# Sharing the transfers' semaphores, and moving the last store's wait behind the section's exit

## The chip, the cores and the metric

The kernel runs on one core of one Trainium2 chip. The metric is the device time of one execution in microseconds (us). A run would be called slow if it were over 1.5% above the fastest of its kernel. The span in a profile is the time from the first to the last instruction of the kernel.

## The reference

```python
def setup_inputs():
    batch, m, k, n = 16, 512, 1024, 768
    return {"x": randn(batch, m, k), "weight": randn(k, n), "sub_value": randn(batch, m, n)}   # float32

def reference(x, weight, sub_value):
    return (np.matmul(x, weight) - sub_value).astype(np.float32)
```

The 8192 rows of `x` make 64 row tiles of 128. Each tile is cast to half precision, transposed (on TensorE, for some tiles on VectorE), multiplied with the weights, and VectorE subtracts `sub_value` from the product in place.

## The kernel before

Everything stands in one hand-synchronized section. Each engine has a list of instructions with waits and increments. SyncE issues all 39 transfers, and each takes a semaphore of its own:

```python
    ctx.enter_context(tc.tile_critical(no_gpsimd_drain=True))
    ...
    for name in ("ident", "idle", "w", "cast", "evac", "pair", "turn", "mul", "finish"):
        counter[name] = tc.alloc_semaphore(name)
    ...
    def issue():
        while todo:
            kind, at, n = todo[0]
            ...
            sem = tc.alloc_semaphore(f"{kind}{at}")
            ...
            if kind == "s":                              # sub_value over rows that were stored
                for t in need:
                    waits.append((landed["o", t], 16))
            ...
            for t in span:
                landed[kind, t] = sem
            sp.add(lambda ...: nc.sync.dma_start(out=here, in_=there), waits, (sem, 16))
```

The last transfers of the list store the output in smaller and smaller pieces, 4, 2, 1 and 1 tiles. At the end SyncE waits for every store, then the section ends:

```python
    for q in (sp, act, dve, pool):
        q.emit(q.ops)
    for t in range(n_mt):
        if t == 0 or landed["o", t] is not landed["o", t - 1]:
            nc.sync.wait_ge(landed["o", t], 16)
```

What follows is made by the framework. At the section's exit SyncE raises a signal, each engine drains and answers, and SyncE waits for the answers. Then comes a barrier of all engines, which GpSimd gathers and releases; GpSimd clears the range of all semaphores that the kernel took; a second barrier ends the program.

## Time and profile before

| | before |
|---|---|
| device time, first runs | 211.04, 211.59, 211.55 us |
| span of the profile | 209.4 us |
| TensorE busy | 198.4 us, 95% |
| share of the main DMA queue | 97.8% |
| last store: issued, landed | 205.43, 207.74 us |
| landing to end of span | 1.62 us |

The page gives the span, each engine's busy time, the busy tenths of 40 slices and the DMA queues. The rows to read for this change are the ones at the very end, by source line: L448 is the final waits, L129 the section's entry and exit, L482 the framework's barriers and the clear. A row by source gives engine, operation and count, then minimum, median and maximum of the duration in ns, then the first and last start in us. A `q` behind an engine's name means its sequencer. These views round starts to 0.1 us. Where this document gives three decimals, they are read from the single records of the same trace.

### The profile page before, as it was taken

The numbers are of one execution on the slowest core, as the hardware profiler recorded it, in microseconds if no ns is written. First come the engines' busy times: TensorE is split into PE (matmuls) and PEld (weight loads), VectorE is DVE, ScalarE is ACT, GpSimd is POOL, SyncE is SP. The second block draws the span as 40 slices with busy tenths as digits, with TensorE's granted clock in tenths as the row PEclk, the third lists the DMA queues.
The fourth block names the chain that finished last, engine by engine and source line by source line (L and its number), as shares of the span: only waits on it lengthen the run. The fifth ranks groups of instructions, "written<-read, shape, count | busy, mean of one in ns | idle before, by whom it ended". The sixth has DMA issues, their size and how long they took to land.

```text
span 209.4 us, 2456 instructions
## 1 busy us (share of the span) xinstructions
PE 198.4 (95%) x1250; PEld 80.4 (38%) x738; DVE 114.0 (54%) x186; ACT 112.9 (54%) x115; POOL 0.7 (0%) x6
## 2 busy tenths in 40 slices
PE   7998799999979999999999999999999999999990
PEld 2432244444333344344344334434434433444430
DVE  0242235106149849929956965992994795332231
ACT  2555665676396274655727629455572750765410
POOL 1000000000000000000000000000000000000000
PEclk9999999999999999999999999999999999999998
DMA  6999999999999999999999999999999999999994
GB/s 200 417 427 425 427 432 434 441 438 423 401 448 417 452 412 429 452 432 424 421 427 452 415 437 448 407 424 446 423 435 441 426 423 426 427 434 432 427 383 171
DMA packets 5626, 87.17 MB, mean 416 GB/s; under 512 B 624, under 2 KB 624, under 8 KB 2032
## 3 DMA queue, kind: packets, MB, share of 16 engines
q1 hardware_dynamic: 5616, 87.03, 97.8%
q8 instruction: 7, 0.11, 0.2%
q14 instruction: 3, 0.02, 0.0%
HBM read 61.87 MB, written 25.17 MB: 416 GB/s over the span
## 4 chain that ended last, share of the span: by engine, by line
PE 80%; DMA 6%; DVE 5%; ACT 4%; SPq 2%; issue 1%; ACTq 0%
PE po_b L175 71%; PE pt_b L289 10%; DMA x_ring<-in_x_dram 6%; DVE xtp_b L316 3%; ACT x_b L271 2%; ACT xt_b L296 1%; DVE so_ring L360 1%; SPq L223 1%; SPq L252 1%; ACT x16p_b L271 0%; SPq L482 0%; ACTq L56 0%; SPq L129 0%
## 5 line engine op out<-in xcount | busy, mean ns | idle before, releaser
L175 PE MATMUL po_b<-w_sb,xt_b 128*128 128x384 f16 x800 | 145.7, 326 | 1.5 <-ACT xt_b L296 1.5
L360 DVE TENSOR_TENSOR so_ring<-po_b,so_ring 128x768 f32<-128x768 f32 x64 | 60.7, 956 | 60.5 <-PE po_b L175 40.2
L296 ACT COPY xt_b<-pt_b 128x1024 f16<-128x1024 f16 x50 | 50.6, 1012 | 73.8 <-PE pt_b L289 73.1
L340 PEld LDWEIGHTS <-xt_b 128*128 128x128 f16 x400 | 39.2, 98 | 58.4 <-issue 52.9
L316 DVE STREAM_TRANSPOSE xtp_b<-x16p_b 32x256 f32<-32x256 f32 x112 | 48.8, 436 | 19.3 <-ACT x16p_b L271 17.4
L289 PE MATMUL pt_b<-ident,x_b 128*128 128x128 f32 x200 | 52.3, 274 | 2.7 <-ACT x_b L271 2.4
L271 ACT CAST x_b<-x_ring 128x1024 f16<-128x1024 f32 x50 | 51.6, 1048 | 5.9 <-DMA x_ring<-in_x_dram 5.9
L289 PEld LDWEIGHTS pt_b<-ident,x_b 128*128 128x128 f32 x200 | 27.6, 141 | 46.3 <-issue 40.4
L175 PE MATMUL po_b<-w_sb,xtp_b 128*128 128x384 f16 x224 | 42.9, 326 | 0.3 <-DVE xtp_b L316 0.3
L271 ACT CAST x16p_b<-x_ring 128x1024 f16<-128x1024 f32 x14 | 14.6, 1046 | 6.8 <-DMA x_ring<-in_x_dram 6.8
L340 PEld LDWEIGHTS <-xtp_b 128*128 128x128 f16 x112 | 11.0, 98 | 13.2 <-issue 11.2
L377 PE MATMUL po_b<-idle_x,idle_w 128*128 128x512 f16 x25 | 8.5, 496 | 1.5 <-DVE idle_x L371 1.5
L226 DVE CAST w_sb<-so_ring 128x768 f16<-128x768 f32 x8 | 4.1, 556 | 10.6 <-DMA so_ring<-in_weight_dram 10.6
L377 PEld LDWEIGHTS po_b<-idle_x,idle_w 128*128 128x128 f16 x25 | 3.0, 122 | 5.2 <-issue 3.0
L271 ACT ACT_TABLE_LOAD x1 | 1.3, 1283 | 0.9 <-SPq L129 0.9
L370 DVE MEMSET idle_w<- 128x64 uint32 x1 | 0.1, 112 | 1.0 <-SPq L129 1.0
L390 PE MATMUL po_b<-idle_x,idle_w 128*128 128x512 f16 x1 | 0.4, 379 | 0.0
L164 POOL TENSOR_SCALAR_AFFINE_SELECT ident<-ident 128x128 f32<-128x128 f32 x1 | 0.3, 292 | 0.1
L371 DVE MEMSET idle_x<- 128x256 uint32 x1 | 0.3, 272 | 0.0
L163 POOL MEMSET ident<- 128x128 f32 x1 | 0.2, 206 | 0.5 <-SPq L129 0.5
L390 PEld LDWEIGHTS po_b<-idle_x,idle_w 128*128 128x128 f16 x1 | 0.1, 98 | 0.2 <-issue 0.2
L471 POOL MEMSET const-bfloat16-1.0<- 128x1 bf16 x1 | 0.1, 102 | 0.0
(3 smaller groups left out, 0.3 us busy)
## 6 DMA issues: line engine op xcount, KB each, us to landing
so_ring<-in_sub_value_dram SPq DMA_DIRECT2D x7, 3072.0 KB, 24.3
out_dram<-so_ring SPq DMA_DIRECT2D x7, 3072.0 KB, 31.2
x_ring<-in_x_dram SPq DMA_DIRECT2D x5, 4096.0 KB, 22.7
x_ring<-in_x_dram SPq DMA_DIRECT2D x2, 2560.0 KB, 26.2
x_ring<-in_x_dram SPq DMA_DIRECT2D x3, 1536.0 KB, 22.4
so_ring<-in_weight_dram SPq DMA_DIRECT2D x4, 768.0 KB, 8.7
x_ring<-in_x_dram SPq DMA_DIRECT2D x3, 512.0 KB, 6.3
so_ring<-in_sub_value_dram SPq DMA_DIRECT2D x1, 1536.0 KB, 26.3
```

Source lines behind the costliest of these rows:

```text
L175: return nc.tensor.add_instruction(mybir.InstMatmult(name=nc.get_next_instruction_name(), engine=full.engine, ins=list(full.ins), outs=lis ...
L223: sp.add(lambda st=st, at=at: nc.sync.dma_start(out=st, in_=w_c[at]), then=(sem, 16))
L226: lambda at=at, r=r, st=st: nc.vector.tensor_copy(out=w_sb[:, at, r], in_=st[:, r]),
L252: sp.add(lambda here=here, there=there: nc.sync.dma_start(out=here, in_=there), waits, (sem, 16))
L271: act.add(lambda: nc.scalar.copy(out=to, in_=x_in), waits, count("cast"))
L289: pe.add(lambda: nc.tensor.transpose(words, from_, ident), waits, count("turn") if last else None)
L296: act.add(lambda: nc.scalar.copy(out=xt_b[:, d], in_=pt_b[:, b]), waits, count("evac"))
L316: dve.add(lambda: nc.vector.transpose(xt[b * Q : (b + 1) * Q, :, a * Q : (a + 1) * Q], x16[a * Q : (a + 1) * Q, :, b * Q : (b + 1) * Q],), ...
L340: pe.add(lambda weights=weights: nc.tensor.ldweights(weights, tile_position=(0, 0)), [w for w in waits if w[0] in ready])
L360: dve.add(lambda: nc.vector.tensor_tensor(out=o, in0=po[:, :, :NS], in1=o, op=mybir.AluOpType.subtract), [(landed["s", mi], 16), (counter[ ...
L377: lambda: nc.tensor.matmul(po_b[:, NPO - 1, 0], idle_w, idle_x, start=True, stop=True),
L390: pe.add(lambda: nc.tensor.matmul(po_b[:, NPO - 1, 0], idle_w, idle_x, start=True, stop=True), [(counter["ident"], 2)])
```

## The change

The intent: use fewer semaphores, so that less has to be cleared at the end, and let the exit's handshake between the engines run while the last store is still under way.

```diff
-    ctx.enter_context(tc.tile_critical(no_gpsimd_drain=True))
+    section = ctx.enter_context(ExitStack())
+    section.enter_context(tc.tile_critical(no_gpsimd_drain=True))
...
+    def lane(tag):
+        for one in lanes:
+            if one["tags"] <= known:
+                break
+        else:
+            one = {"sem": tc.alloc_semaphore(f"lane{len(lanes)}"), "value": 0, "tags": set()}
+            lanes.append(one)
+        one["value"] += 16
+        one["tags"].add(tag)
+        return one["sem"], one["value"]
...
-            sem = tc.alloc_semaphore(f"{kind}{at}")
...
+            sem, value = lane((kind, at))
             for t in span:
-                landed[kind, t] = sem
+                landed[kind, t] = (sem, value)
...
-    for t in range(n_mt):
-        if t == 0 or landed["o", t] is not landed["o", t - 1]:
-            nc.sync.wait_ge(landed["o", t], 16)
...
+    left = [one for one in lanes if not one["tags"] <= known]
+    last = next(one for one in left if of_o[n_mt - 1] in one["tags"])
+    for one in left:
+        if one is not last:
+            nc.sync.wait_ge(one["sem"], one["value"])
+    section.close()
+    with tc.tile_critical(sync_engine=mybir.EngineType.SP, no_gpsimd_drain=True):
+        nc.sync.wait_ge(last["sem"], last["value"])
```

A lane is a semaphore with a running count, and it is taken again only when all its transfers are known to be over; a wait names the count that was reached. The lines that keep `known` (a load is over when its tile was cast, a store when SyncE waited for it, and so on) are left out here. In the program as built, 39 transfer semaphores become 15 lanes, and the range that is cleared shrinks from 54 to 30 semaphores.

More of the change, by code (lines that the diff above doesn't have):

```diff
@@ L201 @@
     staged = {}
+    lanes = []
+    of_x, of_s, of_o = {}, {}, {}
+    known = set()
+    def lane(tag):
[8 more added lines that the diff above has]
+        return one["sem"], one["value"]
     def issue():
+        nonlocal known
         while todo:
@@ L226, in issue @@
                         lambda at=at, r=r, st=st: nc.vector.tensor_copy(out=w_sb[:, at, r], in_=st[:, r]),
-                        waits=[(sem, 16)], then=count("w"),
+                        waits=[(sem, value)], then=count("w"),
                     )
@@ L239, in issue @@
                 waits.append((counter["cast"], max(cast_at[t] for t in need)))
+                last = max(need, key=lambda t: cast_at[t])
+                known |= {tag for t, tag in of_x.items() if t in cast_at and cast_at[t] <= cast_at[last]}
             if kind == "s":
                 for t in need:
-                    waits.append((landed["o", t], 16))
+                    waits.append(landed["o", t])
+                    known.add(of_o[t])
                 for t in span:
@@ L245, in issue @@
                         waits.append((counter["w"], staged.pop(t % NSO)))
+                        known |= {("w", c) for c in w_at if w_at[c] <= waits[-1][1]}
             if kind == "o":
                 waits.append((counter["finish"], max(finish_at[t] for t in need)))
+                known |= {of_s[t] for t in finish_at if finish_at[t] <= max(finish_at[u] for u in need)}
+            sem, value = lane((kind, at))
             for t in span:
-                landed[kind, t] = sem
+                landed[kind, t] = (sem, value)
+                {"x": of_x, "s": of_s, "o": of_o}[kind][t] = (kind, at)
             if kind == "o":
@@ L258, in cast @@
         first = mi - mi % 2
-        waits = [(landed["x", mi], 16)]
+        waits = [landed["x", mi]]
         if first in ON_DVE:
@@ L361, in finish @@
             out=o, in0=po[:, :, :NS], in1=o, op=mybir.AluOpType.subtract
-        ), [(landed["s", mi], 16), (counter["mul"], mul_at[mi])], count("finish"))
+        ), [landed["s", mi], (counter["mul"], mul_at[mi])], count("finish"))
         finish_at[mi] = so_far["finish"]
```

## The prediction

> **What bounds the kernel now.** I read the page first: span, busy shares, the DMA row of the 40 slices, the chain that ended last.
>
> ```profile
> span 209.4 us, 2456 instructions
> ...
> PE 198.4 (95%) x1250; PEld 80.4 (38%) x738; DVE 114.0 (54%) x186; ACT 112.9 (54%) x115; POOL 0.7 (0%) x6
> ...
> DMA  6999999999999999999999999999999999999994
> ...
> q1 hardware_dynamic: 5616, 87.03, 97.8%
> ...
> PE 80%; DMA 6%; DVE 5%; ACT 4%; SPq 2%; issue 1%; ACTq 0%
> ```
>
> The reader is to see two resources full from the second slice to the last but one: TensorE 95% busy, and the DMA engines with packets during 97.8% of the span. The change adds, removes and resizes no transfer and no matmul, so it cannot shorten that body. What it can touch is the last slice, where the DMA row falls to 4.
>
> Next, the waits of the DMA queue in the last 3.5 us and the stores of the last 11 us.
>
> ```profile
> SPq L252 <- DVE so_ring L360: 2.2, 1, 2.2
> SPq L448 <- DMA out_dram<-so_ring: 1.7, 2, 0.9
> ```
> ```profile
> L252 SPq DMA_DIRECT2D out_dram<-so_ring x3: 332/333/333, 200.1 to 205.4; - x3
> ...
> DMA to landing us min/median/max: 2.3/4.0/5.7
> ```
>
> The last store is issued at 205.4 and lands 2.3 us later, at 207.7. SyncE meanwhile waits twice for landings, about 0.9 us each: until the store before the last is there, then until the last is. The last one's own 0.9 us is transfer time: it moves 384 KB, and 393,216 bytes at the page's mean 416 GB/s are 0.95 us.
>
> Then what stands between that landing and the end, by source line from 205.5 us on.
>
> ```profile
> L448 SPq EVENT_SEMAPHORE  x5: 28/28/28, 205.8 to 207.8; - x5
> ```
> ```profile
> L129 SPq EVENT_SEMAPHORE  x3: 17/28/28, 208.0 to 208.2; - x3
> L129 SPq COMPARE_BRANCH  x1: 32/32/32, 207.8 to 207.8; - x1
> ...
> L129 SPq DRAIN  x1: 7/7/7, 208.1 to 208.1; - x1
> L129 SPq NOP  x1: 13/13/13, 208.3 to 208.3; - x1
> ```
> ```profile
> L482 POOLq EVENT_SEMAPHORE  x4: 17/17/17, 208.4 to 209.3; - x4
> L482 POOLq DRAIN  x3: 34/41/128, 208.1 to 209.1; - x3
> L482 SPq DRAIN  x3: 7/7/7, 208.3 to 208.6; - x3
> ...
> L482 POOLq EVENT_SEMAPHORE_RANGE_CLEAR  x1: 331/331/331, 208.7 to 208.7; - x1
> ```
>
> Three things follow the landing, one after another: the section's exit (L129), a barrier of all engines, and GpSimd's clear of all semaphores with a second barrier (L482). The views round starts to 0.1 us; the single records of the same trace are finer, and I use them from here. SyncE: last landing seen 207.759; branch 207.824; exit signal 207.979; its drain 208.068; two waits for the other engines' drains 208.147 and 208.211; NOP 208.278; two drains 208.325 and 208.389. GpSimd: gather 208.421, release 208.499, drain 208.580 (128 ns), clear 208.738 (331 ns), drain 209.103, release 209.259. Span's end 209.364. So **1.605 us** run from 207.759 to the end with no data moving. That is all the change can win.
>
> **What the Trainium skill says.** Perfetto Trace Analysis, section Sequencer-only Instruction (DRAIN, etc): only execution is reported, and the semaphore wait and the propagation of an update are not in the record. The trace agrees: wait records last 28 ns but start 59 to 67 ns apart, and the drain that waits for SyncE's own exit signal starts 89 ns after it. I therefore count from start to start, never by the busy time.
>
> DMA: Bandwidth & Descriptors, section Why a DMA increments its semaphore by 16 and not by 1: two transfers in flight on one semaphore can pass a wait early, since the later one's increments fill the earlier one's count. That is why a lane is reused only after an engine has shown its transfers over. The trace of before, with one semaphore each, cannot show it; it matters for correctness, not for time.
>
> Runtime: NRT & Kernel Launch, the breakdown of the preamble and postamble: it lists a semaphore reset of about 1.5 us for 51 semaphores an engine, outside the kernel. That is 29 ns each. The kernel's own clear took 331 ns for 54, 6.1 ns each, so the page's figure does not carry over and the measurement decides.
>
> The same page, Instruction fetch mechanics: a taken branch out of the fetched window costs a fetch. SyncE's exit branch here was followed 155 ns later by its next instruction, against about 65 ns for plain waits: a small extra, no long stall.
>
> **The change part by part.**
>
> *Body.* Set side by side as built, the two programs have the same instructions in the same order on all engines up to the exit, and the same waits in the same places; only the semaphore's name and the threshold differ. No transfer waits for a lane to come free: if none is known free, a new one is made. Cost 0.
>
> *Fewer semaphores.* The 39 transfer semaphores become 15 lanes in the program as built (the description says 21, and 15 plus the 6 of the section frame is 21). With 9 counters and those 6, the cleared range falls from 54 to 30. If the clear costs the same for each semaphore, 331 x 30/54 = 184 ns, so 147 ns are saved, all on the path. If half of it is a fixed cost, 74 ns. I take 120 ns, an estimate; no second size of the clear is in the trace.
>
> *Final waits.* L448 has five records of two waits each, and the exit branch carries an eleventh. Now seven waits come ahead of the first exit, in three records and the branch, and the eighth, for the last store, behind it. All but the last store have landed before: they are not on the path in either kernel.
>
> *Moved wait.* Before, after the landing (start to start): wait to branch 65, branch to signal 155, signal to drain 89, drain to wait 79, wait to wait 64, wait to NOP 67, NOP to drain 47, drain to drain 64: 630 ns up to the gather. The new second section lives on SyncE alone and keeps most of that behind the landing: the wait, a branch, its own signal, drain, NOP, drain, drain. What leaves the path is only the two waits for the other engines: 64 + 67 = **131 ns**.
>
> *Does the first exit fit ahead of the landing?* The store before the last is seen at 206.844. Then branch +65, signal +155, drain +89, waits +79 and +64, NOP +67, the new entry NOP +80 (a wait for its own signal, as above), waits +47, +65, +65: SyncE stands at the last wait at about 207.62. The last store is seen at 207.759. It fits, with about 0.14 us to spare.
>
> Sum: 0.131 + 0.120 = **0.25 us**, 0.12% of the time. 211.55 - 0.25 = 211.30; but the three runs of before span 211.04 to 211.59, with a mean of 211.39, which suggests a slightly lower centre. I predict **211.2 us**.
>
> **The rivals.**
>
> *The first exit takes the wait's place.* If the two last stores land closer together than 0.78 us, the handshake is no longer hidden, and up to 0.13 us comes back. Against: the last store's transfer alone takes 0.9 us behind a full queue. Time: 211.3.
>
> *The second section costs more than it hides.* Two more sequencer no-ops, another branch, another signal. If the branch behind the landing needs a fetch of its own (155 ns became several hundred), or the other engines get a branch that SyncE's barrier then waits for, the gain is gone: 211.5 or a little above. For: the skill's remark on branches. Against: the exit branch of before, equally to the next block, cost only 155 ns, and the other engines reach the barrier long before SyncE.
>
> *The clear is a fixed cost.* Then 0.13 us is all: 211.3. For: a GpSimd memset of one element still takes 98 to 102 ns. Against: 331 ns is three times as long.
>
> *More is won than the span shows.* The profiled run took 211.14 us for a span of 209.4: 1.8 us lie outside. If part of that grew with the kernel's semaphores, up to some 0.5 us more might go: 210.7. Nothing in the profile speaks for it.
>
> *Sharing delays a transfer or a consumer.* Only if a wait's threshold were later than before; the side by side excludes it.
>
> **Range and chances.** Every rival ends between 210.7 and 211.6, and the spread of the runs, 0.55 us, is twice the expected gain. Range 210.75 to 211.65. Two per cent is 4.2 us, more than twice the whole 1.6 us tail, so within 2% gets 0.975. Faster gets 0.015, slower 0.01 for something unforeseen.
>
> **What would show each step.** In the changed kernel's profile: the clear at 180 to 240 ns instead of 331; SyncE at the last wait before the last store's landing, the other engines' exit drains before it too; about 0.50 us instead of 0.63 from landing to gather; landing to end about 1.35 us instead of 1.6; TensorE's and the DMA queue's busy times unchanged, the last store issued at about 205.4 and landing 2.3 us later. It would be wrong if the clear stayed at 331 ns, if SyncE came to the last wait after the landing, if the second branch cost over 0.2 us, or if the last store's issue moved by more than 0.3 us, which would mean that the body had changed.

## The result, and the profile after

The changed kernel took 210.83 us (median of 4 runs, 210.75 to 211.00), the kernel before 211.37 us (median of 4, 211.04 to 211.59). The ratio is 0.9977, with a 95% interval of 0.9960 to 0.9994. A ratio here is the mean time of one kernel's fast runs over that of the other's in the same rounds, so it is not quite the ratio of the medians. The interval ends just below 1.

The page of the changed kernel:

```profile
span 208.9 us, 2462 instructions
...
PE 197.5 (95%) x1250; PEld 80.1 (38%) x738; DVE 114.0 (55%) x186; ACT 113.0 (54%) x115; POOL 0.7 (0%) x6
...
DMA  6999999999999999999999999999999999999994
...
q1 hardware_dynamic: 5616, 87.03, 97.9%
...
PE 68%; DMA 18%; DVE 5%; SPq 3%; ACT 1%; issue 1%; DVEq 0%; ACTq 0%
```

The instruction counts of the engines, the DMA row and the queue's packets and bytes are the same as before. TensorE's busy time is 0.9 us less, but that is not the change: before_again, the unaltered kernel, has 198.1 us and after_third 198.5. The last line gives a new 18% to the DMA engines, but that is only the way along which the releases were followed back: before_again has the very same line, and the pace of the body is the same. From the start of the 17th subtraction on VectorE to that of the 63rd, 131.212 us pass in the profile before (70.636 to 201.848) and 131.212 us in this one (70.523 to 201.735).

The waits of SyncE in the last 3.5 us, then its stores of the last 11 us:

```profile
SPq L276 <- DVE so_ring L384: 2.2, 1, 2.2
SPq L483 <- DMA out_dram<-so_ring: 0.7, 1, 0.7
SPq L512 <- PEq L512: 0.7, 2, 0.5
SPq L512 <- DMA out_dram<-so_ring: 0.3, 1, 0.3
```
```profile
L276 SPq DMA_DIRECT2D out_dram<-so_ring x3: 332/333/333, 200.0 to 205.3; - x3
...
DMA to landing us min/median/max: 2.3/3.8/5.6
```

The last store still flies 2.3 us. But of the two waits of 0.9 us one has been broken up: only 0.3 us of it is left, at L512. Meanwhile SyncE did the exit. By source line (L483: waits ahead of the exit, L130: first exit, L485: second section, L512: the last wait and the framework):

```profile
L483 SPq EVENT_SEMAPHORE  x3: 27/28/28, 205.7 to 206.5; - x3
```
```profile
L130 SPq EVENT_SEMAPHORE  x3: 17/28/28, 206.7 to 207.0; - x3
L130 SPq COMPARE_BRANCH  x1: 33/33/33, 206.6 to 206.6; - x1
```
```profile
L485 SPq NOP  x2: 13/13/13, 207.1 to 208.0; - x2
L485 SPq EVENT_SEMAPHORE  x1: 17/17/17, 207.8 to 207.8; - x1
L485 SPq DRAIN  x1: 7/7/7, 207.9 to 207.9; - x1
```
```profile
L512 SPq EVENT_SEMAPHORE  x5: 17/28/337, 207.2 to 208.9; - x5
...
L512 POOLq DRAIN  x3: 34/41/99, 206.9 to 208.7; - x3
...
L512 SPq COMPARE_BRANCH  x1: 33/33/33, 207.7 to 207.7; - x1
L512 POOLq EVENT_SEMAPHORE_RANGE_CLEAR  x1: 201/201/201, 208.4 to 208.4; - x1
```

Three things are to be seen. The exit of L130 now stands at 206.6 to 207.0 us, ahead of the landing at 207.627. One wait of L512 has a record of 337 ns: it is the wait for the last store, begun at 207.312. And the clear takes 201 instead of 331 ns, the longest drain of GpSimd, which stands right ahead of it, 99 instead of 128.

From the single records of both traces, in us:

| | before | after | less by |
|---|---|---|---|
| last store issued | 205.434 | 205.319 | 0.115 |
| last store landed | 207.742 | 207.627 | 0.115 |
| landing to GpSimd's gather | 0.679 | 0.513 | 0.166 |
| gather to its drain | 0.159 | 0.159 | 0 |
| drain's start to clear's start | 0.158 | 0.128 | 0.030 |
| clear's start to end of span | 0.626 | 0.496 | 0.130 |
| landing to end | 1.622 | 1.296 | 0.326 |
| span | 209.364 | 208.923 | 0.441 |

So 0.33 us are won behind the landing, and 0.11 us lie ahead of it, where the prediction expected nothing. The medians differ by 0.54 us, more than either.

### The profile page after: what moved, and what is told of

Its sections match the earlier page's. It is cut to its first block, busy times and chain, and to the rows that moved or that the text cites. A ratio compares the mean times of both kernels' runs of the same rounds, so it can differ in the third digit from the quotient of the medians.

```text
span 208.9 us, 2462 instructions
## 1 busy us (share of the span) xinstructions
PE 197.5 (95%) x1250; PEld 80.1 (38%) x738; DVE 114.0 (55%) x186; ACT 113.0 (54%) x115; POOL 0.7 (0%) x6
## 4 chain that ended last, share of the span: by engine, by line
PE 68%; DMA 18%; DVE 5%; SPq 3%; ACT 1%; issue 1%; DVEq 0%; ACTq 0%
PE po_b L176 61%; DMA so_ring<-in_sub_value_dram 18%; PE pt_b L313 7%; DVE xtp_b L340 3%; SPq L276 2%; DVE so_ring L384 2%; SPq L240 1%; ACT xt_b L320 0%; ACT x16p_b L295 0%; ACT x_b L295 0%; SPq L512 0%; DVEq L56 0%; ACTq L56 0%; SPq L130 0%
## 5 line engine op out<-in xcount | busy, mean ns | idle before, releaser
L401 PE MATMUL po_b<-idle_x,idle_w 128*128 128x512 f16 x25 | 7.5, 449 | 1.5 <-DVE idle_x L395 1.5
L414 PE MATMUL po_b<-idle_x,idle_w 128*128 128x512 f16 x1 | 0.4, 379 | 0.0
```

The lines of the kernel that those rows point to most:

```text
L401: lambda: nc.tensor.matmul(po_b[:, NPO - 1, 0], idle_w, idle_x, start=True, stop=True),
L414: pe.add(lambda: nc.tensor.matmul(po_b[:, NPO - 1, 0], idle_w, idle_x, start=True, stop=True), [(counter["ident"], 2)])
```

## The experiments

The theory to test: the two parts add up, both lie behind the last landing, and nothing else is won. The rivals: one part does it all; the clear does not go by the number of semaphores; the exit was not really hidden; sharing makes the body faster. Twelve runs were made, of eight altered kernels and, as controls, of some kernels again, in three sets on three chips, all with correct results. Within a set all share the runs of the kernel before. A time of a whole run scatters by 1 us and more, as much as anything to be found here, so I read the tail from the records and the whole from the mean of the spans.

| run | landing to gather | drain, clear | landing to end | mean span, runs | before in the same set | ratio (95%) |
|---|---|---|---|---|---|---|
| e1_lanes_only | 0.673 us | 99, 201 ns | 1.456 us | 209.40, 6 | 209.56, 11 | 0.9979 (0.9952 to 1.0006) |
| e2_wait_only | 0.518 | 128, 331 | 1.461 | 209.35, 6 | 209.56 | 0.9981 (0.9953 to 1.0009) |
| e3_more90 | 0.683 | 254, 811 | 2.231 | 210.12, 6 | 209.56 | 1.0006 (0.9980 to 1.0033) |
| e4_exposed | 1.317 | 99, 201 | 2.101 | 209.85, 4 | 209.56 | 0.9998 (0.9962 to 1.0033) |
| before_again | 0.679 | 128, 331 | 1.622 | 209.55, 6 | 209.50, 11 | 1.0012 (0.9988 to 1.0035) |
| after_again | 0.514 | 99, 201 | 1.297 | 209.00, 6 | 209.50 | 0.9995 (0.9968 to 1.0021) |
| e6_pool | 0.545 | 106, 203 | 1.338 | 209.0, 1 | 209.50 | one look |
| e7_split | 0.850 | 99, 201 | 1.633 | 209.35, 6 | 209.50 | 0.9995 (0.9981 to 1.0010) |
| e8_two_behind | 0.580 | 99, 201 | 1.366 | 209.18, 6 | 209.66, 11 | 0.9975 (0.9945 to 1.0005) |
| e9_pad24 | 0.513 | 128, 331 | 1.456 | 209.70, 6 | 209.66 | 0.9994 (0.9961 to 1.0026) |
| after_third | 0.513 | 99, 201 | 1.297 | 209.02, 6 | 209.66 | 0.9959 (0.9929 to 0.9989) |
| e1_again | 0.673 | 99, 201 | 1.457 | 209.35, 6 | 209.66 | 0.9976 (0.9949 to 1.0004) |

### One part alone: the lanes (e1_lanes_only)

```diff
-    left = [...]; last = ...
-    for one in left:
-        if one is not last:
-            nc.sync.wait_ge(one["sem"], one["value"])
-    section.close()
-    with tc.tile_critical(sync_engine=mybir.EngineType.SP, no_gpsimd_drain=True):
-        nc.sync.wait_ge(last["sem"], last["value"])
+    for one in lanes:
+        if not one["tags"] <= known:
+            nc.sync.wait_ge(one["sem"], one["value"])
+    section.close()
```

> One part alone: the transfers share lanes (30 semaphores cleared instead of 54), but all waits stand ahead of the only exit, as before. Theory (the two parts add up, each on the path behind the last landing): the clear 201 ns and the GpSimd drain ahead of it 99 ns as in the changed kernel, so 0.16 us less than before between landing and end (1.46 instead of 1.62 us), while landing to gather stays at 0.68 us. Whole time about 0.16 us below the kernel before, ratio 0.9992. Rival A (the moved wait does it all, the clear is a matter of fixed cost): landing to end 1.62 us, ratio 1.000. Rival B (sharing speeds up the body as well): the last store is issued at least 0.1 us earlier than in the kernel before, at 205.3 us or less, and the ratio is 0.998 or less.

GpSimd's rows of this kernel, by source line:

```profile
L508 POOLq DRAIN  x3: 34/41/99, 208.3 to 209.2; - x3
...
L508 POOLq EVENT_SEMAPHORE_RANGE_CLEAR  x1: 201/201/201, 208.9 to 208.9; - x1
```

The clear and the drain are those of the changed kernel, landing to gather is that of the kernel before. The tail is 1.456 us, 0.166 less than before, as expected, and the mean span is 0.16 us less. Rival A falls. Rival B asked for a last store at 205.3 us; it was issued at 205.68, later than before. Its other sign, a ratio of 0.998 or less, was met, but with an interval that reaches beyond 1: inconclusive.

### The other part alone: the moved wait (e2_wait_only)

```diff
 (the kernel before, with its 39 semaphores)
+    section = ctx.enter_context(ExitStack())
...
-        if t == 0 or landed["o", t] is not landed["o", t - 1]:
+        if landed["o", t] is not landed["o", n_mt - 1] and (t == 0 or landed["o", t] is not landed["o", t - 1]):
             nc.sync.wait_ge(landed["o", t], 16)
...
+    section.close()
+    with tc.tile_critical(sync_engine=mybir.EngineType.SP, no_gpsimd_drain=True):
+        nc.sync.wait_ge(landed["o", n_mt - 1], 16)
```

> The other part alone: one semaphore for each transfer as before (54 cleared), but the wait for the last store stands behind the section's exit. Theory: clear 331 ns and drain 128 ns as before; landing to gather 0.51 instead of 0.68 us; landing to end 1.46 us; ratio 0.9992. Rival (the second section costs what it hides): landing to gather 0.63 us or more, landing to end 1.6 us or more, ratio 1.000.

```profile
L486 POOLq DRAIN  x3: 34/41/128, 207.1 to 209.2; - x3
...
L486 POOLq EVENT_SEMAPHORE_RANGE_CLEAR  x1: 331/331/331, 208.9 to 208.9; - x1
```

Here the clear is the old one and landing to gather the new one, 0.518 us. The tail is 0.161 us shorter than before. The two parts alone give 0.166 + 0.161 = 0.327 us; together they gave 0.326. They add up.

### The clear enlarged (e3_more90)

```diff
 (the kernel before)
+    for n in range(90):
+        tc.alloc_semaphore(f"unused{n}")
```

> The suspected cost enlarged: the kernel before with 90 more semaphores taken and never used, so that 144 are cleared instead of 54. Theory (from the two sizes seen, 331 ns for 54 and 201 ns for 30, so 5.4 ns each and 38 ns fixed; the drain ahead of it 128 and 99 ns, so 1.2 ns each): clear 818 ns, drain 237 ns, landing to end 1.62 + 0.49 + 0.11 = 2.22 us, the whole time 0.6 us above the kernel before, ratio 1.0028. Rival (the clear goes by another measure than the range, such as how many of them were raised): clear still about 331 ns, ratio 1.000. Second rival (time outside the span grows with the semaphores too): the whole time rises by clearly more than the span, 1 us or more.

```profile
L484 POOLq DRAIN  x3: 34/41/254, 208.2 to 209.8; - x3
...
L484 POOLq EVENT_SEMAPHORE_RANGE_CLEAR  x1: 811/811/811, 209.0 to 209.0; - x1
```

The clear goes by the number in the range, raised or not: 201 ns for 30, 331 for 54, 811 for 144. That is 5.4 and 5.3 ns each, with about 40 ns fixed. The drain ahead of it went 99, 128 and 254 ns, 1.2 and 1.4 ns each. The tail is 2.231 us where 2.22 was expected, and the mean span is 0.56 us above the kernel before. The rest outside the span did not grow: its median was 1.82 us, in the runs of before in the same set 2.09. The whole time rose by only 0.0006, where 0.0028 was expected, still within the interval.

### Both exits behind the landing (e4_exposed)

```diff
 (the changed kernel)
     for one in left:
-        if one is not last:
+        if True:
             nc.sync.wait_ge(one["sem"], one["value"])
```

> The changed kernel with the last store waited for ahead of the first exit as well, so both exits stand behind the landing. Theory (the first exit of the changed kernel is hidden by the last store's flight): landing to end grows by what SyncE takes from the last wait of the first section to the last wait of the second in the changed kernel, 0.79 us, from 1.30 to about 2.08 us; the time is 0.79 us above the changed kernel and some 0.3 to 0.45 us above the kernel before. Rival (the order of the waits hardly matters, the gain is in the clear): landing to end 1.3 to 1.5 us, no slower than the kernel before.

The waits of SyncE in the last 4.6 us show no landing behind the exit any more, only the two ahead of it:

```profile
SPq L276 <- DVE so_ring L384: 2.3, 1, 2.3
SPq L483 <- DMA out_dram<-so_ring: 1.8, 2, 1.1
SPq L512 <- PEq L512: 0.7, 2, 0.5
```

Landing to gather is 1.317 us instead of 0.513, so 0.80 us of the first exit and the second's entry are hidden in the changed kernel; 0.79 were expected. The mean span is 0.29 us above that of the kernel before (its tail alone is 0.48 above), so a second section that hides nothing costs more than the fewer semaphores bring. The whole times do not resolve this: a ratio of 0.9998, with an interval from 0.9962 to 1.0033.

### Controls: before_again and after_again

> A control: the kernel before, unaltered, measured against itself. Theory (what differs ahead of the last store's issue from run to run is chance): ratio 1.000 within the interval; landing to end 1.62 us again, while the last store's issue falls anywhere between 205.3 and 205.8 us, the spread of the six profiles so far.

> The changed kernel once more, in five rounds. Theory (only the tail is won, 0.33 us): landing to end 1.30 us, ratio 0.9985, so 0.3 us and not the 0.54 us of the first medians; the last store's issue within the spread of the kernel before. Rival (the body gains as well, 0.2 us): ratio 0.9975 or less and the last store issued at 205.35 us or earlier again.

The kernel before against itself gave 1.0012, with no difference shown. Its tail is 1.622 us to the nanosecond, while its last store was issued 0.26 us later than in the first profile. The changed kernel gave 0.9995 this time, with an interval around 1, its tail 1.297 us and its last store at 205.555. Three of its six times were near 212 us although their spans were 208.9 to 209.2: the scatter lay outside the span. So the ratio of one set cannot tell 0.3 from 0.5 us.

### The wait on another engine (e6_pool)

```diff
 (the changed kernel)
-    with tc.tile_critical(sync_engine=mybir.EngineType.SP, no_gpsimd_drain=True):
-        nc.sync.wait_ge(last["sem"], last["value"])
+    with tc.tile_critical(sync_engine=mybir.EngineType.Pool, no_gpsimd_drain=True):
+        nc.gpsimd.wait_ge(last["sem"], last["value"])
```

> The changed kernel with the second section, and so the wait for the last store, on GpSimd, the engine that gathers the barrier. Theory (what stands behind the landing is a fixed chain of sequencer steps, of which GpSimd needs about as many): landing to gather 0.53 us against 0.51 us, clear 31 semaphores in 206 ns, landing to end 1.30 to 1.33 us. Rival (the hop from SyncE to the gathering engine costs): landing to gather 0.43 us or less.

The barrier's gather came at 208.209, 0.545 us after the landing at 207.664, and landing to end is 1.338 us, 0.04 us longer than with SyncE. Both figures of the theory hold within 0.02 us. Moving the wait to the gathering engine gains nothing.

### A version that was to beat both (e7_split)

```diff
 (the changed kernel; the last tile only)
+        for h in range(2):                      # column halves
+            for c in range(n_c):
+                for r in range(2):
+                    ... ldweights, one matmul into po[:, h, :NS] ...
+            dve.add(... out=o[:, h], in0=po[:, h, :NS], in1=o[:, h] ...)
+            sp.add(... nc.sync.dma_start(out=there[:, h], in_=o[:, h]) ...)
```

> A version that may beat both: the changed kernel, whose last tile is multiplied, subtracted and stored in two column halves, each store of 192 KB. The tail that no rearranged wait can touch is the last store's flight: 2.3 us from issue to landing, of which some 0.9 us is its transfer. Theory: the last subtraction takes 0.5 instead of 0.96 us, so the last store is issued 0.45 us earlier (about 204.9 us), and it lands 1.8 to 1.9 instead of 2.3 us later; landing to end stays 1.30 us; together 0.8 to 0.9 us below the changed kernel, ratio to before 0.994 to 0.995. Rival (the flight is a fixed latency, or the extra weight loads hold TensorE up): 2.3 us again from issue to landing, gain 0.45 us or none.

It is no faster than the changed kernel: mean span 209.35 against 209.00 us. Its stores of the last 7 us, the halves at L431:

```profile
L431 SPq DMA_DIRECT2D out_dram<-so_ring x2: 332/332/332, 203.9 to 205.2; - x2
L276 SPq DMA_DIRECT2D out_dram<-so_ring x1: 332/332/332, 203.0 to 203.0; - x1
...
DMA to landing us min/median/max: 2.5/3.3/3.7
```

The last store, half as large, flew 2.5 us instead of 2.3, so half of the rival held: the flight did not shrink. But it is no fixed time either. A landing raises its semaphore in sixteen steps, and fifteen of them were in by 207.331, 2.10 us after the issue; only the last came at 207.700. The store before it has the same late last step (206.855, then 207.225). What makes it late was not separated.

The other loss was not foreseen in the expectation, but is the first rival of the prediction: the two halves landed at 207.225 and 207.700, 0.475 us apart. (The expectation of e8_two_behind below says 0.37 us; that took 207.331, a step of the last store, for the landing of the first half.) The exit, 0.79 us long, no longer fitted between them. SyncE came to its last wait at 208.027, 0.33 us after the landing, and landing to gather was 0.850 instead of 0.513 us. Counted from the start of the 63rd subtraction, the last store was issued 0.40 us earlier than in the changed kernel (3.185 us after it, not 3.584). The longer flight (0.16) and the exposed exit (0.34) used up more than that: the end came 7.284 us after that start, not 7.188.

### The split version mended (e8_two_behind)

```diff
 (the split version)
-    last = next(one for one in left if of_o[n_mt - 1] in one["tags"])
+    halves = {("o", n_mt - 1, 0), ("o", n_mt - 1, 1)}
+    last = [one for one in left if one["tags"] & halves]
...
+        for one in last:
+            nc.sync.wait_ge(one["sem"], one["value"])
```

> The split version with both halves' waits behind the first exit, so that the exit starts when the store before them has landed. Theory (in the split version the exit takes 0.79 us and the two last landings lie only 0.37 us apart, so SyncE came to its last wait 0.33 us after the landing): now SyncE comes to the last wait about 207.55 us, ahead of the landing at about 207.7; landing to gather back from 0.85 to 0.51 us, landing to end from 1.63 to 1.30 us, the span about 0.33 us shorter than the split version's, near 209.0. Rival (the split version lost by its smaller stores alone): landing to gather 0.85 us again.

With both waits behind the exit, landing to gather fell from 0.850 to 0.580 us and the tail from 1.633 to 1.366; the mean span fell by 0.17 us, not by 0.33. SyncE was in place at 207.524, ahead of the landing at 207.739. Of the remaining 67 ns to 0.513, 62 lie between landing and branch, where SyncE now has a second wait to pass, at 207.793. So the exposed exit is shown. As a whole run the version does not beat the changed kernel: 210.99 us median against 210.84 in the same set, spans 209.18 against 209.02. Yet from the start of the 63rd subtraction to the end it takes 7.002 us, where the changed kernel takes 7.188 to 7.190 in its three profiles: the part that the split touches did become 0.19 us shorter. In this profile that start came later (202.103 us against 201.735 to 201.968), for the reason that the next section leaves open.

### What is open: the time ahead of the landing (e9_pad24, after_third, e1_again)

The sixteen runs of the changed kernel, its first four and two sets of six, have spans between 208.8 and 209.2 us, mean 209.0. Less the tail of 1.30 us its last store lands at 207.7 us on average; in the kernel before it lands at about 207.9 (spans of 209.5 and more, less 1.62). That is some 0.2 us that the tail does not explain.

```diff
 (e9_pad24: the changed kernel)
+    for n in range(24):
+        tc.alloc_semaphore(f"unused{n}")
```

> The changed kernel with 24 unused semaphores added, so the clear goes over 54 again as before; the transfers still share lanes, the wait stands behind the exit. Theory (the number cleared is all that sharing is worth): clear 331 ns and drain 128 ns, landing to end 1.46 us as where only the wait was moved; spans 0.16 us above the changed kernel's. Rival (sharing also lets the transfers go earlier, and the last store lands at 207.7 us on average instead of 207.9): spans about 209.15 us on average; if it was chance, about 209.35 us.

> The changed kernel a third time, for what is open: its ten spans so far have a mean of 208.99 us, and less the tail of 1.30 us its last store lands at 207.7 us, 0.2 us earlier than in the kernel before (spans 209.5, less 1.62, so 207.9). If the body is really faster: spans of mean 209.0 us again, 0.5 us under those of the kernel before in the same rounds. If it was chance: 0.33 us under them.

> The lanes alone once more. If sharing itself makes the body faster: the mean span is 0.35 us or more under that of the kernel before in the same rounds (landing at 207.7 us). If it was chance: 0.17 us under it, as the tail of 1.46 us gives.

The tails were as expected in all three: 1.456, 1.297 and 1.457 us. So the number cleared is all that sharing is worth behind the landing, and padding the range back undoes it.

The spans do not settle the rest. In this set two of the eleven runs of the kernel before had spans of 210.7 us, which lift its mean; by medians (209.5 and 209.05) the changed kernel was 0.45 us under it, by means 0.65. So the 0.1 to 0.3 us beyond the tail came back. The lanes alone were 0.31 us under it by means and 0.2 by medians (209.3), after 0.16 us by means in the first set: nearer to chance. The padded kernel, whose instructions differ from the changed kernel's in nothing but semaphore numbers and the range, was not faster than before (209.70, median 209.65, with one run at 210.7), and above both figures that were expected.

Mean spans less tails give the last landing of each. It is 207.9 to 208.0 us in the kernel before, 207.9 with the lanes alone (twice) and with the moved wait alone, 207.7 in the changed kernel and 207.75 in e4_exposed, which have both parts; but 208.2 in the padded kernel, which has both too. So neither part alone brings the landing forward, and both together do not do so in every build. Nor is 0.2 us much: in its control the kernel before differed by as much from itself in the medians of the spans (209.3 against 209.5).

What can be said is where the differences arise. From the 17th subtraction to the start of the 63rd all fourteen profiles took 131.210 to 131.213 us, whatever the kernel, and the start of the 17th lay between 70.52 and 70.94 us: at 70.52, 70.65 and 70.76 in the changed kernel, at 70.64 and 70.90 in the kernel before. So whatever differs ahead of the landing is set in the first 71 us (in the two split kernels the last tile adds its own part), and the two kernels overlap there. Two stretches scatter: the first load landed at 4.69 to 5.16 us, and from the 8th to the 17th subtraction 31.88 to 32.31 us passed; both scatter in unaltered kernels too (31.88 and 32.23 us in the two profiles of the kernel before). Whether it is chance or something of the start that these runs did not isolate stays open.

## Why the prediction was right, and where not

**The bound.** Right. TensorE and the DMA queue have the same shares, and from the 17th to the 63rd subtraction the body takes the same time to 3 ns in 131 us, in all fourteen profiles. The change could only win in the last 1.6 us, and within 2% was safe.

**The body, cost 0.** Right for waits and order. The mean spans show some 0.2 us that the prediction had no term for; its cause is open, as told above.

**Fewer semaphores, 120 ns.** The mechanism was right, the size too small: 130 ns for the clear and 30 ns for the drain ahead of it. Two things were off in the term. I took a value between a fully proportional cost (147 ns) and a half fixed one (74 ns), but only about 40 of the 331 ns are fixed (e3_more90). And I listed the drain's 128 ns without seeing that it goes by the number too.

**The moved wait, 131 ns.** The two waits for the other engines left the path as said, and the measured 166 ns contain 35 more. Of these, 22 lie between landing and branch: 82 ns before (207.742 to 207.824), 60 after (207.627 to 207.687). The other 13 are a few ns in each of the later steps. The second branch was followed by its next instruction after 155 ns, exactly as the first, so the rival of a slow second branch falls.

**The first exit fits.** Right, with more room than said: SyncE stood at the last wait at 207.312, 0.31 us ahead of the landing, not 0.14. The step from the one wait to the other took 0.79 us, as worked out (0.78), but the two landings lay 1.12 us apart in this profile and 0.91 in that of before. That the rival is real where the landings are closer was shown by e4_exposed (0.80 us exposed) and e7_split (0.34 us). Two steps of this part were wrong. The rival was said to bring back up to 0.13 us, but a fully exposed exit cost 0.64 us more than the kernel before (landing to gather 1.317 us against 0.679). And the 0.9 us between the last two landings was called the last store's transfer time: in the twelve profiles that store the last tile whole, this gap is 0.91 to 1.47 us for the same 384 KB, while the flight stays at 2.30 to 2.33 us. So the gap is not the transfer's own time, and the time to spare changes with it from run to run.

**The sum, 0.25 us.** The tail gave 0.33 us. The predicted 211.2 us and the range held, but the measured 210.83 us lies only 0.08 us above the range's lower end, since about 0.2 us of the difference between the medians is not in the tail. (The range began above the 210.7 us of one of its own rivals.) The mechanism gave the 0.33 us; that the rest stayed within the range is owed to the scatter for which the range had been made wide.

**The rivals of a fixed clear and of time outside the span.** Both fell with e3_more90.

## What to carry to other kernels

Look at what stands behind the last landing as a chain of steps, and count start to start: here 1.6 us with no data moving, of which a fifth could be removed. A wait that is not needed until the semaphores are cleared can go behind the exit handshake, but only if its landing comes later than the handshake takes, here 0.8 us after the store before it; smaller last stores can undo that. Each semaphore taken cost 6.6 to 6.7 ns at the end of this kernel, which is worth something by the dozen, and nothing against a 2% mark.

## What the Trainium skill lacked or had wrong

- Perfetto Trace Analysis, section Sequencer-only Instruction (DRAIN, etc): it says that a record starts when all semaphores are satisfied. The wait for the last store, which waits for two semaphores, has a record of 337 ns that starts at 207.312 us, 0.315 us ahead of the landing at 207.627. In the fourteen profiles, 30 records of SyncE for two semaphores hold a real wait (one came over 60 ns after SyncE's previous record). In 23 of them the late one is the first that the trace lists, and the record is 27 to 28 ns long and starts after it. In the other 7 it is the second, and the record contains the wait: 238 to 689 ns.
- The same section names a semaphore's wait and propagation as hidden, without times. In the profiles before and after, start to start, SyncE's waits follow each other after 59 to 67 ns, and its drain follows its own signal after 85 to 89 ns.
- Runtime: NRT & Kernel Launch, the breakdown of the preamble and postamble, has a reset of semaphores outside the kernel only. The clear that a kernel does itself took about 40 ns and 5.3 to 5.4 ns for each semaphore of the range, and the drain ahead of it 1.2 to 1.4 ns for each. The 29 ns for each that the prediction divides out of this page's figure is an estimate, and this clear is far below it.
